# Decoder block on one core: the S1 parts of the up projection move from opx into rows 12 to 15 of R, and four rotating rows of weight operands move into opx

## The chip, the cores and the metric

The kernel runs on one core of one Trainium2 chip. The metric is the device time of one execution in microseconds (us). The kernel before took 1369.95 us, the median of three runs (1369.72 to 1370.99).

## The reference

One layer of a decoder block on 1024 tokens of 1024 channels, in float32: RMSNorm, one combined input projection, two token mixers (a chunked spatial gating and a dilated window attention), their gated sum through `w_out`, a residual, and then the part that the change touches:

```python
h2 = rms_norm(x, ffn_norm_g[layer])
up = h2 @ w_up[layer]                       # 1024 x 1024 by 1024 x 5632
a, val = up[..., :D_FF], up[..., D_FF:]     # D_FF = 2816
a = causal_depthwise_conv(a, conv_w[layer], conv_b[layer])
x = x + (jax.nn.gelu(a, approximate=False) * val) @ w_down[layer]
return rms_norm(x, final_norm_g)
```

## The kernel before, in words

**Arithmetic.** The large products run on the matmul engine (PE) in the type fp32r. Every operand is first split into a high part (a copy rounded to fp32r, made by ScalarE, ACT) and a low part (the operand less its high part, made by VectorE, DVE, or by GpSimd, POOL). This is `to_parts`, lines 170 and 171. A product is then three passes: high by high, low by high, high by low.

The input, output, up and down projections also use seven products of halves in place of eight (P1 to P7), with sums of quarters as operands. On the side of the activations the quarters are A11, A12, A22 and the sums S1 to S4; `LEFT` says which of them a product multiplies: P1 A11, P2 A12, P6 S2, P7 S3, P5 S1, P4 A22, P3 S4.

**Where the operands lie.** R (16 rows), G1 and G0 (8 rows each) are tiles of [128, rows, 1024] in fp32r, in pools opened with `side="right"`. A row holds a high and a low part of 512 columns each. opx (4 rows, line 1587) and lead (3 rows, line 1391) are tiles of the same type in pools without that word; Y, the staging tiles of loaded weights and the temporaries lie in such pools too.

- In the output projection (L1762) opx, lead and rows 12 to 15 of R take turns as the moving operand. opx is read there last in product P4, the last one.
- In the up projection (L1928) the activations are the moving operand: A11 and A12 in G0, A22 and S2 in G1, S3 in rows 0 to 3 of R, S4 in rows 8 to 11, and S1 in opx. They stay for the whole stage. The weights of one block of 128 channels are the stationary operand, 128 x 128 at a time; one product's weights fill one row. A table in `up_row` gives the row: 13, 14, 15, 12 of R for the first ten products, then a ring of eight rows (4, 5, 6, 7, 15, 12, 13, 14), and after the last P2 a ring of rows 4 to 7.
- In the down projection (L2192) both operands lie in R, two rows to a step, in the order of `SLOT_ROWS`: 12, 14, 0, 2, 4, 6, 8, 10.

**The loops.** The up projection takes 22 blocks of channels. Block 0 is multiplied in the plain way (L1908). Blocks 1 to 21 take seven products each, in the order of the list `order`; one product is 12 matmuls (three passes by four slices of 128 channels, `HIGH_FIRST`), each of 128 x 128 by 128 x 512. A DVE addition or an ACT copy takes the result out of PSUM, the conv and the GELU follow on ACT and DVE, the gated product on POOL, and the result goes to DRAM (`gd`).

**What sets the order.** PE's order is written out by hand for the whole kernel. ACT's and DVE's is written by hand in `beginning_up` (the first 23 products, and on to the 37th) and again from the last P2 on; between them a scheduler orders them. `up_ahead(loads, opened)` loads weights and makes operands a few products ahead of their use; `low(n)` emits the next n low parts on DVE. In `beginning_up` the S1 parts are made (`left_parts(UP_ROWS, "S1", ...)`) after the three products P2 of blocks 1 to 3 have been issued to PE, and before the operands with index 6 and up.

Of the kernel before, what the change touches and what calls it, by code (L numbers as in the profile page):

```python
# [94 lines left out]
def block_kernel(  # L95
# [38 lines left out]
    R = rpool.tile([P, 16, 1024], F32R, name="R")  # L134
# [34 lines left out]
    def to_parts(hi, lo, src, lo_eng):  # L169
        nc.scalar.activation(hi, src, AF.Copy)  # L170
        fn = lambda: lo_eng.tensor_tensor(lo, src, f32(hi), ALU.subtract)  # L171
        if written[0] and lo_eng is nc.vector:
            waiting.append(fn)
        else:
            fn()

    def low(n):
        for _ in range(min(n, len(waiting))):
            waiting.pop(0)()
# [52 lines left out]
    def left_parts(rows_of, name, src, part):  # L232

        arena, row = rows_of[name]
        for kt in range(QK):
            t = left[name, kt] = two(arena, row + kt)
            c = part * HALF + kt * P
            hi, lo = (t[:, a].rearrange("p (b t) -> p b t", b=4) for a in range(2))
            to_parts(hi, lo, src[:, :, c : c + P], nc.vector)
# [1074 lines left out]
    for i, (n, name) in enumerate(in_order):  # L1314
# [56 lines left out]
    MIX_ROWS = {  # L1371
        "A11": (G0, 0), "A12": (G0, 4), "A22": (G1, 0), "S2": (G1, 4),
        "S3": (R, 0), "S1": (R, 4), "S4": (R, 8),
    }
# [210 lines left out]
    wp_stack.close()  # L1585
    wq = c_stack.enter_context(tc.tile_pool(name="wq", bufs=4, reuse_waits="tile"))
    opx = wq.tile([P, 4, 1024], F32R, name="opx", bufs=1)
    UP_ROWS = {**MIX_ROWS, "A21": MIX_ROWS["S4"], "S1": (opx, 0)}
    x1d = dram.tile([S, D], F32, name="x1d")
    gd = dram.tile([NFF, P, S], F32, name="gd")  # L1590
    gsum = {n: dram.tile([NK, P, HALF], F32, name=f"g{n}") for n in ("S1", "S2", "S3")}
# [24 lines left out]
    last_p2 = order.index((NFF - 1, "P2"))  # L1616
# [4 lines left out]

    def up_row(ff, name):
        i = order.index((ff, name))
        if i < 10:
            return R, (13, 14, 15, 12)[i % 4 if i < 4 else (i - 4) % 4]
        if i <= last_p2:
            return R, (4, 5, 6, 7, 15, 12, 13, 14)[(i - last_p2 + 3) % 8]
        return R, 4 + (i - last_p2 - 1) % 4

    def up_op(ff, name):  # L1630
        op = row_op(up_row(ff, name))
        free = nc.vector if ff in (1, 4) else nc.gpsimd
        lo_eng = nc.vector if name in ("P2", "P5", "P4") or (ff in LEADS and name == "P1") else free
        weight_op(
            upst[ff, 0], upst.get((ff, 1)), t3s, ff, name, lambda: temp(f"t3_{ff}"),
            op, free, lo_eng,
        )
        ops[ff, name] = op
# [3 lines left out]
    def up_ahead(loads, opened):  # L1642

        while ready["load"] < min(loads, len(order)):
            ff, name = order[ready["load"]]
            if name in ("P1", "P6"):
                up_load(ff, int(name == "P6"))
            ready["load"] += 1
        while ready["op"] < min(opened, len(order)):
            up_op(*order[ready["op"]])  # L1650
            ready["op"] += 1
# [9 lines left out]
    def turn_h(b, bank):  # L1661
# [16 lines left out]
        if b == 3:  # L1678
            left_parts(UP_ROWS, "A11", Y[:, 0:4], 0)
            left_parts(UP_ROWS, "A12", Y[:, 0:4], 1)  # L1680

# [98 lines left out]
    for j, name in enumerate(OSEQ):  # L1780
# [5 lines left out]
        for n in range(4):  # L1786
            s = 4 * j + n
# [60 lines left out]
    def ge_of(ff, h):  # L1848
        if ff == 0:
            return ge_first[h]  # L1850
        return ge1s[ff % 2] if h else ge0s[ff % 4]
# [9 lines left out]
    def begin_taps(cv, src, ff):  # L1861
        nc.scalar.activation(cv, src, AF.Identity, bias=cw(3, ff), scale=cw(2, ff))
# [35 lines left out]
    def plain_product_up(h, which, beside):  # L1898

        name = f"pu_{h}_{which}"  # L1900
        if h or which:
            acc = ps_d.tile([P, HALF], F32, name=name, tag="dn")
        else:
            acc = acc_tile(name)
        for n in range(KT):
            k, kt = n // QK, n % QK
            for i, (w, a) in enumerate(PASSES):
                nc.tensor.matmul(  # L1908
                    acc, plain_up[which, k][:, w, kt, :], left[f"A{h + 1}{k + 1}", kt][:, a, :],
                    start=n == 0 and i == 0,  # L1910
                    stop=n == KT - 1 and i == 2,
                )
            for fn in beside.get(n, ()):
                fn()
        return acc
# [78 lines left out]
    def down_op(s):  # L1994

        j, kt = steps[s]
        row = SLOT_ROWS[s % 8]
        op = R[:, row : row + 2, :].rearrange("p o (a c) -> p o a c", a=2)
        a, *less, b = raw.pop(s)
        for t in less:  # L2000
            nc.vector.tensor_tensor(a, a, t, ALU.subtract)
        if SEQ[j] == "P6":
            nc.sync.dma_start(gsum["S2"][kt], a)
        for o, src in enumerate((a, b)):
            to_parts(op[:, o, 0], op[:, o, 1], src, nc.vector)
        dops[s] = op

    def down_ahead(loads, opened):
        while done["op"] < min(opened, len(steps)):
            down_op(done["op"])  # L2010
            done["op"] += 1
        while done["load"] < min(loads, len(steps)):
            down_load(done["load"])
            done["load"] += 1
# [14 lines left out]
    def beginning_up():  # L2029
# [8 lines left out]
        })  # L2038
        left_parts(UP_ROWS, "A21", s3, 0)
        begin_taps(ge_of(0, 0), gate0, 0)  # L2040
# [3 lines left out]
        value0 = plain_product_up(0, 1, {})  # L2044
        left_parts(UP_ROWS, "A22", Y[:, 4:8], 1)
        up_ahead(7, 3)
# [20 lines left out]
        low(1)  # L2067
        left_parts(UP_ROWS, "S2", Y[:, 0:4], 0)
        for ff in LEADS:
            up_product(ff, "P2")  # L2070
        for fn in (s5, s6, s7):
            fn()
        left_parts(UP_ROWS, "S3", s3, 0)
        low(4)
# [192 lines left out]
    s = 0  # L2267
# [192 lines left out]
```

## Time and profile before

| | us |
|---|---|
| median of three runs | 1369.95 |
| the profiled execution | 1368.7 |
| its span, from the first to the last instruction | 1367.0 |
| PE busy in the span | 1356.0 |
| ACT, DVE, POOL busy | 645.2, 1034.2, 306.4 |
| up projection on PE (blocks 1 to 21) | about 736 to 1150 |
| granted clock of PE (share) | 0.999 |

In rows of the trace, `uP<-opx,R` names the result, then the moving operand's tile and the stationary one's. `up` are the products P1 and P2, `uP` the others. A start-to-start distance on PE is the time that a matmul costs there; a row's own duration also holds the pipeline's depth, and durations of neighbours overlap. `PEld` are the loads of the stationary operand.

### The profile page before, as it was taken

What the parts mean: (1) busy time and instruction counts of PE and PEld (TensorE: products, weight loads), DVE (VectorE), ACT (ScalarE), POOL (GpSimd) and SP (SyncE); (2) the same over time, 40 slices, a digit from 0 to 9 for tenths busy, and PEclk for the clock granted to TensorE, in tenths of its full rate; (3) what the DMA queues carried; (4) which work ended last, traced back from release to release, by engine and by line L of the source; (5) the groups of instructions that cost most, each with busy time, mean ns of one, the idle gap of its engine ahead of it and who ended that gap; (6) DMA issues with size and microseconds to landing.
All of it is one profiled execution on the core that took longest, in us unless ns stands there. A gap on an engine that the chain in (4) does not pass through costs nothing.

```text
span 1367.0 us, 19142 instructions
## 1 busy us (share of the span) xinstructions
PE 1356.0 (99%) x6408; PEld 1126.5 (82%) x6408; DVE 1034.2 (76%) x1878; ACT 645.2 (47%) x1267; POOL 306.4 (22%) x301
## 2 busy tenths in 40 slices
PE   9999999999999999999999999999999999999997
PEld 8877888888888888888888888888888888888886
DVE  6988696777877987759779878676666668676674
ACT  7762455555543325335456344433344335354453
POOL 1123000001320000220011235666555653000002
PEclk9999999999999999999999999999999999999999
DMA  9435453554438995884741133223333327986663
GB/s 344 111 101 175 124 167 105 149 161 126 131 112 281 324 309 181 281 284 148 252 153 57 57 103 133 94 100 123 116 100 108 108 101 263 389 319 216 205 202 123
DMA packets 144577, 236.99 MB, mean 173 GB/s; under 512 B 13920, under 2 KB 57952, under 8 KB 144480
## 3 DMA queue, kind: packets, MB, share of 16 engines
q1 hardware_dynamic: 141952, 231.53, 51.4%
q0 software_dynamic: 1088, 2.10, 0.9%
q10 hardware_dynamic: 1440, 2.16, 0.4%
q8 instruction: 50, 0.82, 0.3%
q14 instruction: 47, 0.39, 0.1%
HBM read 167.77 MB, written 64.29 MB: 170 GB/s over the span
## 4 chain that ended last, share of the span: by engine, by line
PE 88%; DVE 5%; DMA 2%; ACT 2%; issue 1%; POOL 1%; SPq 0%; ACTq 0%; POOLq 0%; DVEq 0%
PE in_P L540 27%; PE uP L1928 17%; PE dn L2192 15%; PE up L1928 7%; PE pa L1401 5%; PE wo_P L1762 5%; PE pu L919 2%; PE pu L1908 2%; PE pb L1401 2%; PE pl L613 1%; PE pp L903 1%; PE sc L864 1%; PE sc L865 1%; DMA X<-in_xt_dram 1%; DVE Y L1866 1%
## 5 line engine op out<-in xcount | busy, mean ns | idle before, releaser
L540 PE MATMUL in_P<-R,G 128*128 128x512 f32 x1008 | 244.1, 394 | 0.0
L540 PEld LDWEIGHTS in_P<-R,G 128*128 128x128 f32 x1008 | 185.5, 188 | 37.0 <-ACT G L312 0.2
L2192 PE MATMUL dn<-R 128*128 128x512 f32 x924 | 209.6, 389 | 0.0
L2192 PEld LDWEIGHTS dn<-R 128*128 128x128 f32 x924 | 173.4, 188 | 36.0
L170 ACT ACTIVATE R<-up 128x512 fp32r<-128x512 f32 x130 | 78.4, 626 | 118.7 <-DVE up L279 40.6
L312 ACT ACTIVATE G<-wr 128x512 fp32r<-128x512 f32 x126 | 78.9, 628 | 98.7 <-PE in_P L540 66.2
L540 PE MATMUL in_P<-G,G 128*128 128x512 f32 x504 | 122.0, 393 | 0.1
L1928 PE MATMUL uP<-G,R 128*128 128x512 f32 x504 | 121.4, 390 | 0.7 <-DVE Y L1949 0.5
L1928 PE MATMUL uP<-R 128*128 128x512 f32 x504 | 121.1, 389 | 0.0
L1928 PE MATMUL up<-G,R 128*128 128x512 f32 x504 | 120.5, 390 | 0.0
L1928 PEld LDWEIGHTS uP<-G,R 128*128 128x128 f32 x504 | 94.4, 188 | 21.3 <-DVE Y L1949 0.9
L1928 PEld LDWEIGHTS up<-G,R 128*128 128x128 f32 x504 | 94.6, 188 | 20.1
L1928 PEld LDWEIGHTS uP<-R 128*128 128x128 f32 x504 | 94.6, 188 | 19.6
L540 PEld LDWEIGHTS in_P<-G,G 128*128 128x128 f32 x504 | 93.0, 188 | 19.3 <-DVE G L454 0.5
L313 DVE TENSOR_TENSOR G<-wr,G 128x512 fp32r<-128x512 f32 x126 | 88.2, 700 | 26.1 <-ACT G L312 24.9
L171 POOL TENSOR_TENSOR R<-up,R 128x512 fp32r<-128x512 f32 x55 | 82.9, 1509 | 63.0 <-ACT R L170 62.3
L171 DVE TENSOR_TENSOR R<-up,R 128x512 fp32r<-128x512 f32 x75 | 65.9, 882 | 19.4 <-ACT R L170 19.1
L170 ACT ACTIVATE R<-db 128x512 fp32r<-128x512 f32 x77 | 48.1, 626 | 57.8 <-PE dn L2192 45.8
L171 DVE TENSOR_TENSOR R<-db,R 128x512 fp32r<-128x512 f32 x77 | 53.6, 699 | 26.5 <-ACT R L170 26.4
L1401 PE MATMUL pa<-R,G 128*128 128x512 f32 x288 | 67.9, 389 | 0.0
L970 POOL TENSOR_TENSOR ld<-ld,w 128x256 f32<-128x256 f32 x16 | 11.2, 722 | 235.5 <-DVE w L958 235.5
L1401 PEld LDWEIGHTS pa<-R,G 128*128 128x128 f32 x288 | 54.1, 188 | 11.2
(286 smaller groups left out, 2438.5 us busy)
## 6 DMA issues: line engine op xcount, KB each, us to landing
up<-in_w_up_dram SPq DMA_DIRECT2D x44, 512.0 KB, 3.6
wr<-in_w_in_dram SPq DMA_DIRECT2D x42, 512.0 KB, 4.3
dA<-gd SPq DMA_DIRECT2D x55, 256.0 KB, 5.1
wd<-in_w_down_dram SPq DMA_DIRECT2D x44, 256.0 KB, 4.9
wT<-wd SPq DMA_DIRECT2D x44, 256.0 KB, 3.7
dS<-gS SPq DMA_DIRECT2D x44, 256.0 KB, 4.2
db<-wT SPq DMA_DIRECT2D x44, 256.0 KB, 4.6
gd<-Y SPq DMA_DIRECT2D x42, 256.0 KB, 2.0
```

Of the source, the lines that this page charges most:

```text
L170: nc.scalar.activation(hi, src, AF.Copy)
L171: fn = lambda: lo_eng.tensor_tensor(lo, src, f32(hi), ALU.subtract)
L312: lambda: nc.scalar.activation(op[:, 0], src, AF.Copy),
L313: lambda: nc.vector.tensor_tensor(op[:, 1], src, f32(op[:, 0]), ALU.subtract),
L540: nc.tensor.matmul(acc, op[:, w, kt, :], left[LEFT[name], kt][:, a, :], start=opened and i == 0, stop=i == len(HIGH_FIRST) - 1, skip_group ...
L613: nc.tensor.matmul(lead_banks[b][:, cs], raw_x[h, kt][:, a, c * P : (c + 1) * P], lead_op(kt, w, cs), start=kt == 0 and p == 0 and cs.star ...
L919: nc.tensor.matmul(pu[:, h * HD : (h + 1) * HD], self.pT[:, i, :], vt[:, h * HD : (h + 1) * HD], start=i % n == 0, stop=i % n == n - 1,)
L1401: nc.tensor.matmul(acc, unit[a][kt // 4][:, kt % 4, :], two(R, 8 * h + kt)[:, b, :], start=n == 0 and i == 0, stop=n == len(kts) - 1 and i ...
L1762: nc.tensor.matmul(acc, left[LEFT[name], kt][:, a, blk * P : (blk + 1) * P], out_ops[s][:, w, :], start=name not in SHARED and kt == 0 and ...
L1908: nc.tensor.matmul(acc, plain_up[which, k][:, w, kt, :], left[f"A{h + 1}{k + 1}", kt][:, a, :], start=n == 0 and i == 0, stop=n == KT - 1 ...
L1928: nc.tensor.matmul(acc, op[:, w, kt, :], left[LEFT[name], kt][:, a, :], start=opened and i == 0, stop=i == len(HIGH_FIRST) - 1, skip_group ...
L2192: nc.tensor.matmul(accs[blk], dops[s][:, 0, a, blk * P : (blk + 1) * P], dops[s][:, 1, w, :], start=SEQ[j] not in CONTINUES and kt == 0 an ...
```

## The change

S1's four rows go to R 12 to 15. The weight operands that rotated through R 12 to 15 go to opx, but for the first four (P1 of blocks 1 to 3 and P2 of block 1), which are made before S1 and keep rows 13, 14, 15, 12. The first two steps of the down projection, whose operands are made while S1 is still needed, take opx.

```diff
-    UP_ROWS = {**MIX_ROWS, "A21": MIX_ROWS["S4"], "S1": (opx, 0)}
+    UP_ROWS = {**MIX_ROWS, "A21": MIX_ROWS["S4"], "S1": (R, 12)}
...
     def up_row(ff, name):
         i = order.index((ff, name))
+        if i < 4:
+            return R, (13, 14, 15, 12)[i]
         if i < 10:
-            return R, (13, 14, 15, 12)[i % 4 if i < 4 else (i - 4) % 4]
+            return opx, (1, 2, 3, 0)[(i - 4) % 4]
         if i <= last_p2:
-            return R, (4, 5, 6, 7, 15, 12, 13, 14)[(i - last_p2 + 3) % 8]
+            n = (i - last_p2 + 3) % 8
+            return (opx, (3, 0, 1, 2)[n - 4]) if n >= 4 else (R, 4 + n)
         return R, 4 + (i - last_p2 - 1) % 4
...
         row = SLOT_ROWS[s % 8]
-        op = R[:, row : row + 2, :].rearrange("p o (a c) -> p o a c", a=2)
+        slot = opx[:, 2 * s : 2 * s + 2, :] if s < 2 else R[:, row : row + 2, :]
+        op = slot.rearrange("p o (a c) -> p o a c", a=2)
```

No engine's instructions change their order; the same instructions name other tiles, and a few wait for other things. (Lines behind the edit move by three or four: L1928 becomes L1931, L2192 becomes L2196.) On PE, in the middle of the up projection, seven products in a row of blocks 5 and 6 before (`G_77` is G0, `G_76` is G1; behind the arrow stands the moving operand, then the stationary one, and one name where both are the same tile):

```order
931 L1928 MATMUL uP_5_7571<-G_76,R 128x512 x12
932 L1928 MATMUL up_7587<-G_77,R 128x512 x12
933 L1928 MATMUL uP_5_7605<-R 128x512 x12
934 L1928 MATMUL uP_5_7624<-opx,R 128x512 x12
935 L1928 MATMUL up_7587<-G_77,R 128x512 x12
936 L1928 MATMUL uP_5_7605<-G_76,R 128x512 x12
937 L1928 MATMUL uP_5_7624<-R 128x512 x12
```

and the same seven now:

```order
931 L1931 MATMUL uP_5_7571<-G_76,opx 128x512 x12
932 L1931 MATMUL up_7587<-G_77,opx 128x512 x12
933 L1931 MATMUL uP_5_7605<-R 128x512 x12
934 L1931 MATMUL uP_5_7624<-R 128x512 x12
935 L1931 MATMUL up_7587<-G_77,R 128x512 x12
936 L1931 MATMUL uP_5_7605<-G_76,R 128x512 x12
937 L1931 MATMUL uP_5_7624<-R,opx 128x512 x12
```

The fourth row is P5: its moving operand goes from opx to R. The stationary operand goes from R to opx in three of the seven. Over the whole stage no matmul moves opx any more (252 did), and 840 of the 1764 take their weights from it.

On ACT, where the S1 parts are made (`<-Y ... x4` and the rows around it, with the semaphores each waits for), before:

```order
584 L170 ACTIVATE G_76<-Y 128x512 [waits DVE_49]
585 L170 ACTIVATE G_76<-Y 128x512 x3
586 L170 ACTIVATE R<-own 128x512 x4
587 L170 ACTIVATE opx<-Y 128x512 x4
588 L170 ACTIVATE R<-up_1_6597 128x512 [waits DVE_49,Activation_49]
589 L170 ACTIVATE R<-t_1_7002 128x512 [waits PE_49,Activation_49]
```

and now:

```order
584 L170 ACTIVATE G_76<-Y 128x512 [waits DVE_49]
585 L170 ACTIVATE G_76<-Y 128x512 x3
586 L170 ACTIVATE R<-own 128x512 x4
587 L170 ACTIVATE R<-Y 128x512 [waits PE_49,Activation_49]
588 L170 ACTIVATE R<-Y 128x512 x3
589 L170 ACTIVATE opx<-up_1_6597 128x512 [waits DVE_49]
590 L170 ACTIVATE opx<-t_1_7002 128x512
```

The first S1 part now waits for PE (the product P2 of block 1 reads row 12), and the two weight operands behind it (P6 and P7 of block 1) lose waits, P7's that for PE. On DVE the low parts of the operands with index 4, 5 and 6 lose a wait for PE as well, and so do the parts of the down projection's steps 8 and 9 on ACT and DVE; one low part on POOL gains a wait for a DMA that was issued earlier.

At the border of the up and the down projection the first 24 matmuls of the down projection (two steps of 12, `dn<-R` before) have both operands in opx; from the third step on both lie in R as before.

## The prediction, as written before the changed kernel ran

> **What bounds the kernel.** I read the page's busy times first, then the chain of work that ended last, then what PE waited for.
>
> ```profile
> span 1367.0 us, 19142 instructions
> PE 1356.0 (99%) x6408; PEld 1126.5 (82%) x6408; DVE 1034.2 (76%) x1878; ACT 645.2 (47%) x1267; POOL 306.4 (22%) x301
> ...
> PE 88%; DVE 5%; DMA 2%; ACT 2%; issue 1%; POOL 1%; SPq 0%; ACTq 0%; POOLq 0%; DVEq 0%
> ```
>
> ```profile
> PE uP L1928 <- DVE Y L1949: 0.5, 1, 0.5
> PE in_P L540 <- DVE ones L2339: 0.4, 1, 0.4
> PE avt L1000 <- ACT pT L909: 0.3, 1, 0.3
> PE uP L1928 <- ACT R L170: 0.2, 1, 0.2
> ```
>
> PE is busy for 1356.0 of 1367.0 us and holds 88% of the chain. In the up projection (L1928) it waits for others 0.5 + 0.2 = 0.7 us in all. So the stage lasts as long as PE takes for its 1764 matmuls. A change there counts by what it does to one matmul, or if it makes an operand late.
>
> So the next view is PE's groups with shapes kept apart (a group's busy time over its count is what one matmul takes of PE):
>
> ```profile
> L1928 PE MATMUL uP<-G,R 128*128 128x512 f32 x504 | 121.4, 390 | 0.7 <-DVE Y L1949 0.5 <-ACT R L170 0.2
> L1928 PE MATMUL uP<-R 128*128 128x512 f32 x504 | 121.1, 389 | 0.0
> L1928 PE MATMUL up<-G,R 128*128 128x512 f32 x504 | 120.5, 390 | 0.0
> L1928 PE MATMUL uP<-opx,R 128*128 128x512 f32 x252 | 62.0, 394 | 0.0
> ```
>
> Three groups of equal shape stand at 121.4 / 504, 121.1 / 504 and 120.5 / 504 = 0.239 to 0.241 us. The fourth, whose moving operand lies in opx, stands at 62.0 / 252 = 0.246 us. These are the 21 products P5. A group's busy time counts overlaps at its ends, so I take the price from start times. PE in order of time, one row to a product, at two places of the stage 288 us apart:
>
> ```profile
> 816.07 2.88 PE L1928 MATMUL uP<-R 128*128 128x512 f32 x12
> 818.79 2.95 PE L1928 MATMUL uP<-opx,R 128*128 128x512 f32 x12
> 821.58 2.90 PE L1928 MATMUL up<-G,R 128*128 128x512 f32 x12
> 824.32 2.88 PE L1928 MATMUL uP<-G,R 128*128 128x512 f32 x12
> 827.04 2.88 PE L1928 MATMUL uP<-R 128*128 128x512 f32 x12
> ```
>
> ```profile
> 1103.74 2.88 PE L1928 MATMUL uP<-R 128*128 128x512 f32 x12
> 1106.46 2.96 PE L1928 MATMUL uP<-opx,R 128*128 128x512 f32 x12
> 1109.26 2.90 PE L1928 MATMUL up<-G,R 128*128 128x512 f32 x12
> 1111.99 1.30 PE L1928 MATMUL uP<-G,R 128*128 128x512 f32 x5
> ```
>
> A product from R or G takes 818.79 - 816.07 = 2.72 us, and so does the next but one, 827.04 - 824.32 = 2.72. P5 takes 821.58 - 818.79 = 2.79, and the product behind it 824.32 - 821.58 = 2.74. The second place gives 2.72, 2.80 and 2.73. So a P5 costs 0.07 us itself and 0.02 in the product behind it, as if starts lagged a little behind the work: 0.09 us too much. This is 0.07 / 12 = 0.0058 us for one matmul.
>
> Is it opx, or is it P5? The output projection answers: there opx and lead hold weights, as the moving operand, beside rows of R in the same products.
>
> ```profile
> 681.20 0.86 PE L1762 MATMUL wo_P<-opx,R 128*128 128x512 f32 x3
> 681.89 2.23 PE L1762 MATMUL wo_P<-R 128*128 128x512 f32 x9
> 683.96 2.96 PE L1762 MATMUL wo_P<-opx,R 128*128 128x512 f32 x12
> 686.75 0.86 PE L1762 MATMUL wo_P<-R 128*128 128x512 f32 x3
> ```
>
> Twelve matmuls that move opx take 686.75 - 683.96 = 2.79 us, as P5 does. Twelve with three from opx take 683.96 - 681.20 = 2.76. Other data, other products, the same price: it goes with the tile that is moved.
>
> **The change part by part.** PE's instructions and their order stay; only tiles and waits change.
>
> *S1 in R.* 252 matmuls move R in place of opx. 21 products times 0.09 us: 1.89 us less. By the groups alone it would be (0.246 - 0.240) x 252 = 1.5, without the product behind.
>
> *Weights in opx.* 840 matmuls of the stage now take their stationary operand from opx. No row of before has 512 columns moving against a stationary operand from opx or a tile of its kind, so the price is bounded. Below: nothing, or a gain for which no row speaks. Above: if reading there costs the stationary side what it costs the moving side, 0.0058 us each plus 0.02 at the end of each of 17 runs of such products, 840 x 0.0058 + 17 x 0.02 = 5.2 us. The nearest row is that of the transposes, whose stationary operand `xn` lies in a pool of the same side as opx:
>
> ```profile
> 721.40 1.03 PE L1666 MATMUL ht<-ident,xn 128*128 128x128 f32 x8
> 722.19 0.94 PE L1762 MATMUL wo_P<-opx,G 128*128 128x512 f32 x3
> 722.97 0.86 PE L1762 MATMUL wo_P<-R,G 128*128 128x512 f32 x3
> ```
>
> From 721.40 to 722.97 there lie eight transposes and three matmuls that take 3 x 0.233 = 0.70, so 0.87 / 8 = 0.11 us for a load from `xn` and its matmul together. In the up projection 0.227 us are there for each load (2.72 / 12), and it runs beside the matmul ahead of it. With half of that free, I take 0 and keep both ends for the range.
>
> [...]
>
> *The down projection's first two steps.* 24 matmuls move opx: 24 x 0.0058 + 0.02 = 0.16 us more.
>
> *The new wait.* ACT's first S1 part waits for P2 of block 1. ACT, DVE and PE at that place:
>
> ```profile
> 749.08 2.18 ACT L170 ACTIVATE R<-own 128x512 fp32r<-128x512 f32 x4
> 751.16 2.18 ACT L170 ACTIVATE opx<-Y 128x512 fp32r<-128x512 f32 x4
> ```
>
> ```profile
> 756.14 2.49 DVE L171 TENSOR_TENSOR opx<-Y,opx 128x512 fp32r<-128x512 f32 x4
> ```
>
> ```profile
> 742.75 10.14 PE L1928 MATMUL up<-G,R 128*128 128x512 f32 x44
> 752.72 0.62 PE L1908 MATMUL pu<-R 128*128 128x512 f32 x2
> ...
> 769.04 2.96 PE L1928 MATMUL uP<-opx,R 128*128 128x512 f32 x12
> ```
>
> Two products of 2.72 us stand between P2 of block 1 and 752.72, so it has ended issuing at 747.3. ACT arrives at 751.16, 3.9 us later: the wait costs nothing. Queued behind it are the other S1 parts and operands 6 and 7; S1 is first moved at 769.04, 10 us after DVE has made its low parts (756.14 + 2.49). Writing to R costs ACT what writing to opx does, 2.18 for four. The lost waits concern operands that are ready early, and gain nothing. POOL's wait is for a DMA that lay ahead of it anyway.
>
> *What is late next.* PE comes 0.09 us sooner to each later product. Near the start of the ring operands are made only just in time:
>
> ```profile
> 801.96 2.90 PE L1928 MATMUL up<-G,R 128*128 128x512 f32 x12
> 805.04 1.20 PE L1928 MATMUL uP<-G,R 128*128 128x512 f32 x4 [0.19 <-ACT R L170]
> ```
>
> That product takes 805.04 - 801.96 = 3.08, 0.34 over the 2.74 of one behind a P5: PE waits for ACT. What the three P5 ahead of it save (0.27) can be lost here, as far as ACT doesn't itself go by PE. I charge half, 0.13.
>
> **The sum.** -1.89 + 0 + 0.16 + 0.13 = -1.6 us. The profiled execution took 1368.7 us, a span of 1367.0 and 1.7 around it; it would take 1367.1. It lies 1.25 under the median of the runs; the same -1.6 from 1369.95 gives **1368.4 us**, -0.12%. Its own range is 1367.3 to 1369.3, from the spread of before's runs.
>
> **Rivals.** (1) *The weights pay what S1 saves*, slower. If what costs time is that PE's two operands lie on different sides, or if reading from opx costs the weights as well, the 840 matmuls pay up to 5.2 us: -1.89 + 5.2 = +3.3, and 1373.3 us; the 24 of the down projection change little. For it: the slow matmuls of before all had a mixed pair, opx or lead against R or G, and no row shows the other mixture. Against it: the transposes' 0.11 us. It decides from 1.89 / 840 = 0.0023 us for one matmul.
>
> (2) *Nothing changes.* The price is one of P5's data or of its place in the order, or PE's gain ends in later waits for ACT: 1369.95 + 0.16, about 1370. The 2.79 of the output projection speaks against the first, the 0.7 us of waits against the second.
>
> (3) *More than the sum*, if the wait at 805 goes because the lost waits let operands come sooner: 0.34 more, and the charge of 0.13 gone, 1367.9. Those operands were ready early, which speaks against it.
>
> **How the numbers follow.** The forecast has 0.55, rival 1 has 0.28 (its price is bounded only from afar), rival 2 has 0.10, rival 3 has 0.03, and 0.04 is for what I don't see. About 0.2% of 1370, 2.7 us, is what a measurement of this kernel can tell from no change: faster is under 1367.2, slower over 1372.7. Faster has 0.04 of the forecast, its far low end, and half of the unseen: 0.06. Slower has 0.26 of rival 1 and the other half: 0.28. The rest, 0.51 + 0.10 + 0.03 + 0.02 of rival 1, is 0.66 for within. The range from 1367.3 to 1374.0 takes in the forecast, rivals 2 and 3, and rival 1 with the spread of the runs (0.7) above it.
>
> **What would show it.** Right: a P5 (now `uP<-R`, among them `uP<-R,opx`) takes 2.72 us from start to start, and so does a product that reads its weights from opx (`uP<-G,opx`, `up<-G,opx`); the first two steps of the down projection take 2.79 each; the up projection ends 1.5 us sooner against its start. Wrong: products with weights in opx take 2.79 (rival 1), a P5 still takes 2.79 (rival 2), or PE shows new waits for ACT or DVE in the first 70 us of the ring. A loaded stationary operand that shows up in PE's start times at all would undo the forecast.

## The result and the profile after

The changed kernel takes 1372.51 us (median of 20 runs, 1370.83 to 1374.22), the kernel before 1369.83 (20 runs, 1367.99 to 1372.03). The ratio is 1.0017, with a 95% interval of 1.0011 to 1.0023: slower by about 2.3 us by the ratio (the two medians lie 2.7 apart), where 1.6 less was forecast. The profiled execution's span grew from 1367.0 to 1369.7 us.

The page of the changed kernel, its busy times and the chain that ended last:

```profile
span 1369.7 us, 19137 instructions
PE 1359.7 (99%) x6408; PEld 1127.7 (82%) x6408; DVE 1034.4 (76%) x1878; ACT 646.3 (47%) x1267; POOL 312.7 (23%) x301
...
PE 93%; DVE 3%; DMA 2%; ACT 1%; issue 1%; SPq 0%; POOL 0%; ACTq 0%; DVEq 0%; POOLq 0%
```

and all that PE waited for:

```profile
PE warm L391 <- POOL ident masks.py:199: 1.7, 1, 1.7
PE in_P L540 <- DVE ones L2343: 0.4, 1, 0.4
PE avt L1000 <- ACT pT L909: 0.3, 1, 0.3
PE rs_bc L423 <- DVE YC L417: 0.2, 1, 0.2
```

PE is busy for 3.7 us more, its share of the chain rose from 88% to 93%, and the 0.7 us of waits in the up projection are gone: none of the four rows belongs to that stage. There no engine makes PE wait; its own matmuls take longer. Which ones, the groups by shape and tile show (result, moving operand, stationary operand):

```profile
L1931 PE MATMUL uP<-R 128*128 128x512 f32 x396 | 93.7, 389 | 0.0
L1931 PE MATMUL uP<-R,opx 128*128 128x512 f32 x360 | 87.3, 395 | 0.0
L1931 PE MATMUL up<-G,R 128*128 128x512 f32 x276 | 65.9, 389 | 0.0
L1931 PE MATMUL uP<-G,opx 128*128 128x512 f32 x252 | 62.0, 395 | 0.0
L1931 PE MATMUL uP<-G,R 128*128 128x512 f32 x252 | 60.7, 390 | 0.0
L1931 PE MATMUL up<-G,opx 128*128 128x512 f32 x228 | 55.9, 395 | 0.0
```

The three groups with weights from opx (360 + 252 + 228 = 840 matmuls) stand at 0.243 to 0.246 us, the three with weights from R at 0.237 to 0.241. PE in order of time, one row to a product, says it without overlaps (these matmuls' own durations average 389 to 395 ns, while 2.72 us for twelve puts the next start 227 ns later):

```profile
844.36 2.89 PE L1931 MATMUL uP<-G,R 128*128 128x512 f32 x12
847.08 2.95 PE L1931 MATMUL uP<-R,opx 128*128 128x512 f32 x12
849.87 2.95 PE L1931 MATMUL uP<-G,opx 128*128 128x512 f32 x12
852.67 2.95 PE L1931 MATMUL up<-G,opx 128*128 128x512 f32 x12
855.46 2.94 PE L1931 MATMUL uP<-R,opx 128*128 128x512 f32 x12
858.24 2.89 PE L1931 MATMUL uP<-R 128*128 128x512 f32 x12
860.96 1.29 PE L1931 MATMUL up<-G,R 128*128 128x512 f32 x5
```

From start to start the four products with weights in opx take 2.79, 2.80, 2.79 and 2.78 us, the ones around them 2.72. The border to the down projection holds the row that decides between explanations:

```profile
1152.98 5.61 PE L2196 MATMUL dn<-opx 128*128 128x512 f32 x24
1158.43 1.75 PE L2196 MATMUL dn<-R 128*128 128x512 f32 x7
```

Here both operands lie in opx, and 24 matmuls take 1158.43 - 1152.98 = 5.45 us, 2.72 for twelve. So opx is not slow to read. In this stage a matmul pays when one operand lies in opx and the other in R or G.

### The profile page after: what moved, and what is told of

Read it like the earlier page. It is cut to its first block, busy times and chain, and to the rows that moved or that the text cites. A ratio compares the mean times of both kernels' runs of the same rounds, so it can differ in the third digit from the quotient of the medians.

```text
span 1369.7 us, 19137 instructions
## 1 busy us (share of the span) xinstructions
PE 1359.7 (99%) x6408; PEld 1127.7 (82%) x6408; DVE 1034.4 (76%) x1878; ACT 646.3 (47%) x1267; POOL 312.7 (23%) x301
## 4 chain that ended last, share of the span: by engine, by line
PE 93%; DVE 3%; DMA 2%; ACT 1%; issue 1%; SPq 0%; POOL 0%; ACTq 0%; DVEq 0%; POOLq 0%
PE in_P L540 27%; PE uP L1931 21%; PE dn L2196 15%; PE up L1931 8%; PE pa L1401 5%; PE wo_P L1765 5%; PE pu L919 2%; PE pu L1911 2%; PE pb L1401 2%; PE pl L613 1%; PE pp L903 1%; PE sc L864 1%; DMA X<-in_xt_dram 1%; PE sc L865 1%; PE pm L727 1%; DMA C<-in_x_dram 1%
## 5 line engine op out<-in xcount | busy, mean ns | idle before, releaser
L2196 PE MATMUL dn<-R 128*128 128x512 f32 x900 | 204.2, 389 | 0.0
L2196 PEld LDWEIGHTS dn<-R 128*128 128x128 f32 x900 | 168.9, 188 | 35.1
L1931 PE MATMUL uP<-R 128*128 128x512 f32 x396 | 93.7, 389 | 0.0
L1931 PE MATMUL uP<-R,opx 128*128 128x512 f32 x360 | 87.3, 395 | 0.0
L1931 PEld LDWEIGHTS uP<-R 128*128 128x128 f32 x396 | 74.3, 188 | 15.5
L1931 PEld LDWEIGHTS uP<-R,opx 128*128 128x128 f32 x360 | 67.8, 188 | 15.8
L170 ACT ACTIVATE R<-up 128x512 fp32r<-128x512 f32 x70 | 43.0, 627 | 65.6 <-PE uP L1931 23.9
L1931 PE MATMUL up<-G,R 128*128 128x512 f32 x276 | 65.9, 389 | 0.0
L170 ACT ACTIVATE opx<-up 128x512 fp32r<-128x512 f32 x60 | 37.0, 628 | 56.3 <-DVE up L279 18.6
L540 PE MATMUL in_P<-G 128*128 128x512 f32 x252 | 61.7, 392 | 0.4 <-DVE ones L2343 0.4
L1931 PE MATMUL uP<-G,opx 128*128 128x512 f32 x252 | 62.0, 395 | 0.0
```

Source lines behind the costliest of these rows:

```text
L540: nc.tensor.matmul(acc, op[:, w, kt, :], left[LEFT[name], kt][:, a, :], start=opened and i == 0, stop=i == len(HIGH_FIRST) - 1, skip_group ...
L1931: nc.tensor.matmul(acc, op[:, w, kt, :], left[LEFT[name], kt][:, a, :], start=opened and i == 0, stop=i == len(HIGH_FIRST) - 1, skip_group ...
L2196: nc.tensor.matmul(accs[blk], dops[s][:, 0, a, blk * P : (blk + 1) * P], dops[s][:, 1, w, :], start=SEQ[j] not in CONTINUES and kt == 0 an ...
```

## The experiments

Two theories are left for the mixed pair. **A, the offset:** in the built program R, G0 and G1 start at 2016 bytes modulo 2048 in each partition, and lead and opx at 1888. Rows are 4096 bytes long and slices 512 bytes, so any pair within R and G stands at an offset of 0 modulo 512, and opx against R or G stands 128 bytes short of that. **B, the sides:** PE pays when its operands lie in pools of different sides. The experiments move opx, or lead and opx, by some bytes; the instructions and their order stay. An offset is given as the stationary operand's address less the moving one's.

**Padding ahead of opx (e1, e2).** In the change (e1) and in the kernel before (e2):

```diff
+    wq.tile([P, 32], F32, name="pad", bufs=1)
     opx = wq.tile([P, 4, 1024], F32R, name="opx", bufs=1)
```

Expected of e1:

> The change, with 128 bytes of padding ahead of opx, so that opx starts at the same place as R, G0 and G1 modulo 2048 bytes (before and in the change it starts 128 bytes short of that). Theory A (the pair's offset: a matmul pays when its two operands' addresses in a partition differ by something that is no multiple of 512): the products with weights in opx take 2.72 us from start to start in place of 2.79, the stage loses 5.2 us against the change, and the output projection's matmuls that move opx lose their price too, about 1 us; time 0.996 to 0.997 of before times the change's 1.0017, which is 0.997 to 0.998 of before. Theory B (the sides: PE pays when one operand lies in a pool of the left side and the other in one of the right): nothing changes, 2.79, ratio 1.0017.

Measured: 1368.0 us, ratio 0.9982 (0.9973 to 0.9991) to the kernel before. PE in order of time:

```profile
848.21 2.88 PE L1932 MATMUL uP<-G,opx 128*128 128x512 f32 x12
850.93 2.88 PE L1932 MATMUL up<-G,opx 128*128 128x512 f32 x12
853.65 2.88 PE L1932 MATMUL uP<-R,opx 128*128 128x512 f32 x12
856.37 2.88 PE L1932 MATMUL uP<-R 128*128 128x512 f32 x12
```

Every product takes 2.72 us, weights in opx or not. The stage loses 3.8 us against the change (416.12 to 412.30), less than the 5.2 expected: with PE faster, its waits in the stage are back, 0.7 for DVE and 0.2 for ACT. Expected of e2:

> The kernel before, with the same 128 bytes ahead of opx; S1 stays in opx. Theory A: P5 takes 2.72 us in place of 2.79 and the product behind it 2.72 in place of 2.74, 21 x 0.09 = 1.9 us less, and about 1 us less in the output projection, where opx is moved: ratio 0.998. Theory B: P5 stays at 2.79, ratio 1.000.

Measured: 1367.88 us, ratio 0.9983 (0.9974 to 0.9993).

```profile
816.36 2.88 PE L1929 MATMUL uP<-R 128*128 128x512 f32 x12
819.08 2.88 PE L1929 MATMUL uP<-opx,R 128*128 128x512 f32 x12
821.80 2.88 PE L1929 MATMUL up<-G,R 128*128 128x512 f32 x12
824.52 2.88 PE L1929 MATMUL uP<-G,R 128*128 128x512 f32 x12
```

P5 takes 2.72 in place of 2.79 with S1 still in opx, and the product behind it 2.72. The stage loses 1.6 us of the 1.9 expected, and PE's waits in it grew from 0.7 to 0.9. opx stayed on its side in both kernels, so B is out: 128 bytes of padding alone took P5 from 2.79 to 2.72. The lengths of the stages, from PE's first matmul of each to the first of the next (the down projection to its last):

| | output projection to up | up projection | down projection |
|---|---|---|---|
| before | 96.20 | 413.85 | 209.21 |
| the change | 96.26 | 416.12 | 209.23 |
| e1, the change, opx padded | 95.71 | 412.30 | 209.21 |
| e2, before, opx padded | 95.73 | 412.24 | 209.21 |

With the offset gone the two placements take equally long (412.30 and 412.24). The change's 2.3 us stand in the up projection alone. The output projection, which moves opx too, gains 0.5, about half of the 1 that was expected; the waits of e1 and e2 both have a new one there, 0.4 us of PE for ACT's `xn` (L1727 and L1724), that neither before nor the change has.

**Rows at several offsets (e3, e4, e7, e8).** Longer rows put each row of opx at its own offset, and one product's weights fill one row. Four products in a run take rows 3, 0, 1, 2. For e4 (e7 has 24 and 1032 for the two numbers, e8 has 80 and 1040, e3 has rows of 1040 and no pad):

```diff
-    opx = wq.tile([P, 4, 1024], F32R, name="opx", bufs=1)
+    wq.tile([P, 64], F32, name="pad", bufs=1)
+    opx = wq.tile([P, 4, 1056], F32R, name="opx", bufs=1)[:, :, :1024]
```

> The change, with 256 bytes ahead of opx and rows 128 bytes longer: rows 0 to 3 stand at +128, +256, +384 and +512 bytes against R's. Theory A: rows 0 and 2 2.79 us, row 3 2.72, row 1 tells whether the period is 256 (2.72) or 512 (2.79 or more). The down projection's first two steps have both operands in opx, 128 bytes apart: A says 2.79, though both lie on one side. Theory B: all four rows 2.79, the two steps 2.72 as in the change.

Measured (a single run, 1371.12 us), the rows in the order +512, +128, +256, +384, then weights from R again, and the down projection's first two steps:

```profile
1001.48 2.89 PE L1932 MATMUL uP<-R,opx 128*128 128x512 f32 x12
1004.21 2.96 PE L1932 MATMUL uP<-G,opx 128*128 128x512 f32 x12
1007.00 2.92 PE L1932 MATMUL up<-G,opx 128*128 128x512 f32 x12
1009.76 2.96 PE L1932 MATMUL uP<-R,opx 128*128 128x512 f32 x12
1012.56 2.91 PE L1932 MATMUL uP<-R 128*128 128x512 f32 x12
...
1152.45 5.75 PE L2197 MATMUL dn<-opx 128*128 128x512 f32 x24
1158.04 10.15 PE L2197 MATMUL dn<-R 128*128 128x512 f32 x44
```

The row at +512 takes 2.73, +128 takes 2.79, +256 2.76, +384 2.80. The two steps with both operands in opx, now 128 bytes apart, take 5.59 us, where they took 5.45 at one offset: a pair in one tile pays as well. So neither the side nor the tile decides, which is A.

> The change, with opx's rows 64 bytes longer, so that rows 0 to 3 stand at -128, -64, 0 and +64 bytes against R's rows (modulo 512). Theory A: products with weights in row 2 take 2.72 us, in row 0 2.79, and rows 1 and 3 tell whether 64 bytes matter (2.72 or up to 2.79). Theory B: all four rows 2.79. The first two steps of the down projection have both operands in opx, 64 bytes apart: 2.72 for B; for A 2.72 or 2.79, as rows 1 and 3.

Measured (a single run, 1369.9 us), rows in the order +64, -128, -64, 0, then R:

```profile
1000.43 2.96 PE L1931 MATMUL uP<-R,opx 128*128 128x512 f32 x12
1003.23 2.95 PE L1931 MATMUL uP<-G,opx 128*128 128x512 f32 x12
1006.02 2.92 PE L1931 MATMUL up<-G,opx 128*128 128x512 f32 x12
1008.78 2.89 PE L1931 MATMUL uP<-R,opx 128*128 128x512 f32 x12
1011.51 2.65 PE L1931 MATMUL uP<-R 128*128 128x512 f32 x11
```

2.80 at +64, 2.79 at -128, 2.76 at -64 and 2.73 at 0. 64 bytes short cost less (2.76) than 64 beyond (2.80), which nobody had expected. In the first two steps of the down projection 24 matmuls took 5.52 us, 2.76 for twelve; there the stationary operand lies in the first row of a pair and the moving one in the second, so the offset is again 64 short.

> The change, with 96 bytes ahead of opx and rows 32 bytes longer: rows 0 to 3 at -32, 0, +32 and +64 bytes against R's. Theory A: row 1 2.72 to 2.73 us, row 3 2.80 as 64 bytes cost so far; rows 0 and 2 between or at the same level tell how fine the offset counts (64 bytes short cost 0.03, 64 bytes beyond 0.08).

Measured (a single run, 1372.67 us), rows in the order +64, -32, 0, +32, then R:

```profile
1002.54 2.96 PE L1932 MATMUL uP<-R,opx 128*128 128x512 f32 x12
1005.34 2.96 PE L1932 MATMUL uP<-G,opx 128*128 128x512 f32 x12
1008.14 2.92 PE L1932 MATMUL up<-G,opx 128*128 128x512 f32 x12
1010.90 2.96 PE L1932 MATMUL uP<-R,opx 128*128 128x512 f32 x12
1013.69 2.66 PE L1932 MATMUL uP<-R 128*128 128x512 f32 x11
```

2.80 at +64, 2.80 at -32, 2.76 at 0, 2.79 at +32. So 32 bytes cost as much as 128 did (2.79 at -128 in e3). The first two steps of the down projection, here 32 short, took 5.60 us. The 2.76 at offset 0 I take for no price of that row but for lateness of its first matmuls behind the slow product at -32, as the product behind a P5 took 2.74 in before, and in e4 weights from R behind the row at +384 took 2.75 (to the next start, 1015.31); behind the row at +32 in e7 they took 2.72 (to 1016.41). That is an estimate: no view of e7 splits this product. The next run splits one at +256.

> The change, with 320 bytes ahead of opx and rows 64 bytes longer: rows 0 to 3 at +192, +256, +320 and +384 bytes against R's. Theory A with a period of 512: row 1 2.76 us and row 3 2.79 to 2.80, as 256 and -128 cost so far; rows 0 and 2 lie above 2.72 too. With a period of 256 row 1 would be at 2.72, which the earlier run speaks against.

Measured (a single run, 1373.95 us), rows in the order +384, +192, +256, +320:

```profile
1003.83 2.96 PE L1932 MATMUL uP<-R,opx 128*128 128x512 f32 x12
1006.62 2.96 PE L1932 MATMUL uP<-G,opx 128*128 128x512 f32 x12
1009.42 2.90 PE L1932 MATMUL up<-G,opx 128*128 128x512 f32 x12
1012.16 2.96 PE L1932 MATMUL uP<-R,opx 128*128 128x512 f32 x12
1014.96 2.91 PE L1932 MATMUL uP<-R 128*128 128x512 f32 x12
```

2.79 at +384, 2.80 at +192, 2.74 at +256 and 2.80 at +320. The same view with only the last seven matmuls of the product at +256:

```profile
1010.57 1.75 PE L1932 MATMUL up<-G,opx 128*128 128x512 f32 x7
1012.16 0.40 PE L1932 MATMUL uP<-R,opx 128*128 128x512 f32 x1
```

Seven take 1.59 us, 0.227 each, as with no offset (2.72 / 12 in e1); the five ahead of them took 1.15, 0.230 each. In e3 the product at -64 does not settle:

```profile
1007.17 1.77 PE L1931 MATMUL up<-G,opx 128*128 128x512 f32 x7
1008.78 0.39 PE L1931 MATMUL uP<-R,opx 128*128 128x512 f32 x1
```

Seven take 1.61 us, 0.230 each, so its 2.76 is a price of its own. The down projection's first two steps, in e8 64 short again, took 5.50 us, near e3's 5.52. So my reading of e4 in that expectation, 2.76 as a price of 256, was wrong: at 256 the last seven matmuls run as at 0. All other offsets tried cost 0.03 to 0.08 us for twelve matmuls (2.76 to 2.80, against 2.72 to 2.73).

**Padding ahead of lead (e5, e6).** The version to which this points: lead and opx both on R's offset, in the kernel before (e5) and in the change (e6). One pad does it, as opx lies behind lead and moves with it.

```diff
+    leadp.tile([P, 32], F32, name="pad", tag="pad")
     lead = leadp.tile([P, 3, 1024], F32R, name="lead", tag="lead")
```

> The kernel before, with 128 bytes ahead of lead, so that lead and opx both start where R, G0 and G1 do modulo 2048. Theory A (the pair's offset): all of what the opx padding gave, 1.9 us less in the up projection and 0.5 in the output projection by the runs so far, and the 36 matmuls that move lead lose their 0.006 us each and what follows them, 0.3 us more: ratio 0.998. Theory B (sides) is out by the runs before; if only opx's own place counted, lead would add nothing.

> The change with the same 128 bytes ahead of lead. Theory A: within 0.1% of the kernel before with that padding, ratio 0.998, since without the offset it no longer matters which of the two operands lies in opx. If taking weights from opx had a price of its own besides the offset, the 840 matmuls would show it: over 0.9985, and products with weights in opx over 2.72 us.

Measured: e5 1368.61 us, ratio 0.9990 (0.9981 to 0.9999); e6 1368.64, ratio 0.9988 (0.9979 to 0.9997). Both beat the kernel before, by less than expected (0.998), and by so little that the intervals end just under 1. For e6, a ratio over 0.9985 had been named as a sign that weights from opx have a price of their own. It came, but the other sign did not: products with weights in opx take 2.72 us in e6's trace, and its up projection is no longer than e5's. In the stages the gain is there: 95.51 and 95.47 us for the output projection, 0.2 less than with opx padded alone, and 412.53 and 412.39 for the up projection. The rest lies ahead of these stages, where nothing was changed: e5's output projection starts at 641.5 us, that of before at 640.2, and over all traces of this case that start lies anywhere from 640.1 to 642.7. Whether lead adds anything to the whole time is not settled; the intervals of e1, e2, e5 and e6 overlap. That e5 and e6 agree speaks again for the offset as the only price of weights from opx.

## Why the prediction was wrong, point by point

*S1 in R: right.* P5 takes 2.72 us where its weights lie in R (860.96 - 858.24), as was said, and the gain was there to be had: e2, which cures P5 by other means, shortens the stage by 1.6 us (413.85 to 412.24), with P5 and the product behind it at 2.72 each. Of the missing 0.3, 0.2 went the way the prediction charged for: PE, sooner at the tight places, waited longer there (0.9 in place of 0.7).

*Weights in opx: wrong, and this is the step that failed.* The prediction bounded their price from 0 to 5.2 us and put "With half of that free, I take 0". The runs show the upper end: 70 products at 2.79 in place of 2.72 make 4.9 us. The transposes' row told how long a load and its matmul take together (0.11 us), and from that the weights were taken to be free: an estimate, which no row of before showed. That was the wrong thing to bound: at offset 0 weights from opx are free indeed (2.72 in e1), and the price belongs to the pair of operands, whichever of the two is moved out of step (P5 of before 2.79, weights in opx 2.79). I had asked "is it opx, or is it P5?", and the rows answered "opx" only because every slow row that I had read had its partner in R or G.

*The down projection's first two steps: wrong.* 0.16 us were charged; with both operands at one offset they cost nothing (5.45 us for 24).

*The new wait: right.* ACT and PE of the changed kernel at that place:

```profile
751.60 2.18 ACT L170 ACTIVATE R<-Y 128x512 fp32r<-128x512 f32 x4
```

```profile
741.62 6.29 PE L1931 MATMUL up<-G,R 128*128 128x512 f32 x27
747.74 5.75 PE L1931 MATMUL up<-G,opx 128*128 128x512 f32 x24
```

PE had issued P2 of block 1 by 747.74, and ACT's row has no idle time ahead of it.

*What is late next: the other way round.* A slower PE comes later to the tight place at 805 and no longer waits there. The second tight place, at 863.20 in before (0.46 us for DVE), loses its wait as well. The 0.7 us of waits that the stage had are gone.

*The sum by what was measured:* 4.9 for the weights, less 1.89 for S1, less 0.7 of waits: +2.3 us. The stage grew by 416.12 - 413.85 = 2.27. The terms are each a little rough and their errors nearly cancel: from start to start the four products at the two tight places (from 801.96 and from 859.84 in before) took 1.30 us more than 2.72 each, and 0.46 in the change, where 0.13 are the weights' price, so about 1.0 of waiting went away; products whose own weights lie in R, behind those with weights in opx, add about 0.2 to the 4.9.

*The rivals.* Rival 1 had the mechanism's form (a mixed pair), the price of 0.0058 us for a matmul and, but for the waits, its size: 1373.3 against 1372.51. The stated range holds the measured time only because rival 1 was let into it; the forecast's own range ended at 1369.3. In hindsight the chance of rival 1, 0.28, was too low, and its first reason, different sides, was wrong as well: with opx still on its side and 128 bytes further, the mixed pairs take 2.72 (e1, e2). The sentence against it leant on a row of another kind. That every slow pair read in before was mixed had been written down, and should have weighed more than the transposes, which had no pair of 512 columns in fp32r. (It holds for the rows read in the up and the output projection; in the input projection twelve matmuls between smaller ones of L727 took 2.83, from 100.17 to 103.00 in before, with neither operand in opx or lead.)

What stays open: why an offset costs anything, why 256 is as good as 0 (seven in 1.59 in e8), why 64 short costs less than 64 beyond, and whether other shapes or types pay it. No run tells either whether what counts is a matmul's own two operands, or its moving operand and the weights that are loaded beside it for the next (in before the loads of the P5 at 818.79 begin at 818.57, 188 ns each): in these runs the two differ only at the borders of products.

## What to carry to other kernels

Where PE never waits, compare start-to-start distances of matmuls of one shape across tiles: a difference like the one here (2.79 against 2.72 us for twelve, 3%) is worth a look at where its two operands start in the partition. Before moving an operand to cure a slow matmul, ask which pairs the move creates; here it cured 252 and made 840. A pad that sets two pools on the same offset did more than the move: 0.9982 and 0.9983 of the time, against 1.0017.

## What the runs showed of the hardware that was not expected

In twelve matmuls of 128 x 128 by 128 x 512 in fp32r, with operand addresses in a partition apart by this much modulo 512 bytes (stationary less moving; +512 took 2.73 in e4 and 0 took 2.73 in e3, -128 took 2.79 in e3 and +384 2.80 in e4, which is why they share rows):

| offset, bytes | us for twelve | run |
|---|---|---|
| 0 | 2.72 to 2.73 (behind a slow product 2.74 in before, 2.75 in e4, 2.76 in e7) | all |
| 256 | 2.74 in e8, its last seven in 1.59 (0.227 each, as at 0); 2.76 in e4 | e4, e8 |
| 448 (-64) | 2.76 (seven in 1.61) | e3; in the down projection e3, e8 (5.52, 5.50 for 24) |
| 128, 384 | 2.78 to 2.80 | before, the change, e3, e4, e8 |
| 32, 64, 192, 320, 480 | 2.79 to 2.80 | e3, e7, e8 |

It made no difference whether the moving operand was out of step (P5 before, 2.79) or the stationary one (the change, 2.79), or whether both lay in one tile (e4, 5.59 for 24).
